# A longer landing delay in the model that orders a hybrid layer's instructions

## The chip, the cores and the metric

The kernel runs on one core of a Trainium2 chip. Its time is the device time of one execution in microseconds; the times before are three executions with a median of 1792.1 us (1790.23 to 1797.07).

## The reference

One layer of a streaming encoder on a sequence of 1024 rows of width 2048, all in float32:

```python
u = einsum('bsd,de->bse', h, w_in)            # one input projection, 6752 columns
q, k, v, z_attn, q_idx, k_idx, w_idx, z_ssd, xbc, dt_raw = split(u)
# group A: a token indexer scores the admissible keys, each query keeps the 256 best
logits = relu(einsum('bqhd,bsd->bqhs', q_idx, k_idx))
score  = where(admissible, einsum('bqhs,bqh->bqs', logits, w_idx), -inf)
sel    = top_k(score, 256)
o_attn = softmax_attention(q, k[sel], v[sel]) * silu(z_attn)
# group B: state-space mixer in chunks of 64 rows, behind a causal convolution of 4 taps
o_ssd  = ssd_mixer(conv(xbc), z_ssd, dt_raw)
sub = einsum('bse,ed->bsd', concat(o_attn, o_ssd), w_out)
h   = layer_norm(alpha * h + sub) * ln_g + ln_b
```

## The kernel before

Matrix products are made in three passes: each float32 operand is split into a high part, rounded to the type fp32r (`xh`, `wh`), and the rest (`xl`, `wl`), and TensorE adds high x high, high x low and low x high. ScalarE writes the high part and VectorE (at times GpSimd) the low part. So each 128x512 tile of raw weights (`wr`) or of x (a tile `u`) takes a transfer, a pass on ScalarE and a pass on VectorE before its matmuls. The two halves of the sequence (512 rows each) go through a Strassen-like scheme of seven products for most of the input projection and for the whole output projection; sums of blocks are formed on VectorE and GpSimd, or by accumulating transfers, and some go through scratch in HBM and come back.

The main stream is a list of weight pieces in fixed order (`units`): the indexer columns, products of the first half, the second, then the output projection (`emit_t`, `emit_s`, `emit_o`). A piece feeds 12 matmuls as a rule. Beside it run tasks: Python generators for rope, indexer scores, top-k search, attention (`t_kv`, `t_attn`: load a piece of q, split it, score, softmax, gate), the state-space mixer (`t_ssd`), splits (`t_w` for weights, `t_x` for x), evacuations, residual sums and the layer norm (`t_lnstat`, `t_ln_one`, `t_ln_b`). A task yields a `Need`: on which engines its next step works, which events it waits for and which buffers it takes.

Nothing in this looks at the chip. While the program is written out, class `Sim` keeps a clock for each engine (`clk`: PE, V, A, G, SP, D for the transfers) and for each tile the times at which its writes and reads end. Whenever the main stream is about to go on, `Flow.pump` looks through the tasks by priority and places the first step that `Flow.ready` allows (lines 442 to 461): the end of its previous step, its events and its buffers must lie behind the clocks of the engines that it needs, with 200 ns of allowance, or 300 ns of margin ahead of TensorE's clock. For that test a transfer ends at the time that `Sim.dma` returns. Engines run their instructions in the order so written, and semaphores keep it right whatever the times are; the model decides only the order. Buffers are handed out by the same clocks (`avail`, `new`, `free`): 10 for raw weights, 4 each for the split ones, 16 each for `xh` and `xl`, 30 of the common kind `u`, of which at most 8 (`NXR`) hold raw x. Weights are split up to 3 pieces ahead (`WAHEAD`) and loaded up to 15 pieces ahead.

Nearly all transfers go out on SP's queue, in the order written; accumulating ones go out on GpSimd's. All instructions are recorded from one helper, so they all carry line 327; tiles tell them apart. In `Sim.dma` a transfer starts 400 ns after its issue or when the transfer clock D is free, keeps D busy for its bytes, and lands a fixed time after that:

## Time and profile before

| | before |
|---|---|
| median of three executions | 1792.1 us |
| profiled execution, its own time | 1794.32 us |
| its span, first to last instruction | 1791.9 us |
| mean granted TensorE clock | 0.972 |
| instructions | 26153 |
| moved by transfers | 430.88 MB, mean 240 GB/s |
| SP's queue, GpSimd's queue | 406.14 MB, 23.07 MB |

The profile shows one execution. Busy time is given by engine (PE is TensorE, PEld its weight loads, DVE VectorE, ACT ScalarE, POOL GpSimd, SP the engine that issues most transfers). A wait is put down to what ended it; a landing is the time at which a transfer's semaphore tells that its data is there. The granted clock is the share of TensorE's full clock.

### The profile page before, as it was taken

The page shows a single profiled execution, that of the slowest core. Times are in us where ns is not written, and L with a number is a line of the kernel's source. Part 1 is how long each engine was busy: PE and PEld are TensorE (multiplying, and loading weights), DVE is VectorE, ACT ScalarE, POOL GpSimd, SP SyncE. Part 2 cuts the span into 40 slices and gives each one's busy share as a digit, 9 for nine tenths or more (in the row PEclk, how much of TensorE's full clock was granted, in tenths as well). Part 3 has the DMA queues.
Part 4 walks back from the last instruction along what each step waited for, and adds up shares of the span by engine and source line. Part 5 has one row for each costly group of instructions (what it writes and reads, how often), then busy time and mean ns, then how long its engine had stood idle before and what let it go on. Part 6 is the DMA issues. An engine that isn't in the chain of part 4 may idle for free. (4 is left out here: it accounts for less than half of the span.)

```text
span 1791.9 us, 26153 instructions
## 1 busy us (share of the span) xinstructions
PE 1656.9 (92%) x7989; PEld 1351.7 (75%) x7989; DVE 1389.1 (78%) x3072; ACT 986.1 (55%) x1920; POOL 231.3 (13%) x300
## 2 busy tenths in 40 slices
PE   7999989999989989889889999999999999899991
PEld 6888867877867878677677888877887788677871
DVE  6888564568899879899776768699886878887775
ACT  6656776555655498876842356465665433333341
POOL 3201012000101000000120223101110000000132
PEclk9999999999999999999899999999999999999996
DMA  9589877596367689987989797686657986767998
GB/s 294 159 299 359 210 223 202 178 311 159 99 222 215 212 274 281 292 240 220 309 240 292 227 295 223 202 286 204 207 179 246 352 285 203 239 194 236 338 244 169
DMA packets 271885, 430.88 MB, mean 240 GB/s; under 512 B 29184, under 2 KB 86912, under 8 KB 271232
## 3 DMA queue, kind: packets, MB, share of 16 engines
q1 hardware_dynamic: 259072, 406.14, 69.0%
q0 software_dynamic: 12672, 23.07, 9.0%
q8 instruction: 63, 1.03, 0.2%
q14 instruction: 78, 0.64, 0.1%
HBM read 337.77 MB, written 131.17 MB: 262 GB/s over the span
## 5 line engine op out<-in xcount | busy, mean ns | idle before, releaser
L327 PE MATMUL pj<-xh,wh 128*128 128x512 f32 (+1 forms) x1520 | 601.1, 395 | 28.2 <-ACT wh L327 25.5
L327 PE MATMUL pj<-xh,wl 128*128 128x512 f32 (+1 forms) x1520 | 591.0, 389 | 20.6 <-DVE wl L327 20.4
L327 PE MATMUL pj<-xl,wh 128*128 128x512 f32 (+1 forms) x1520 | 587.5, 387 | 0.8 <-DVE xl L327 0.4
L327 ACT ACTIVATE wh<-wr 128x512 fp32r<-128x512 f32 (+1 forms) x488 | 298.4, 622 | 236.2 <-PE o L327 79.6
L327 DVE TENSOR_TENSOR wl<-wr,wh 128x512 fp32r<-128x512 f32 (+1 forms) x462 | 314.3, 689 | 143.4 <-ACT wh L327 134.8
L327 PEld LDWEIGHTS pj<-xh,wl 128*128 128x128 f32 x1520 | 290.8, 191 | 89.7 <-DVE wl L327 32.8
L327 PEld LDWEIGHTS pj<-xh,wh 128*128 128x128 f32 x1520 | 291.5, 192 | 85.8 <-ACT wh L327 31.2
L327 PEld LDWEIGHTS pj<-xl,wh 128*128 128x128 f32 x1520 | 291.6, 192 | 52.3 <-DVE xl L327 1.4
L327 PE MATMUL a<-u,u 128*128 128x512 f32 (+3 forms) x776 | 181.6, 355 | 17.4 <-DVE u L327 6.4
L327 DVE TENSOR_TENSOR u<-u,u 128x512 f32<-128x512 f32 (+7 forms) x255 | 156.9, 627 | 48.3 <-ACT u L327 33.6
L327 ACT ACTIVATE u<-u 128x512 f32<-128x512 f32 (+4 forms) x209 | 116.5, 576 | 100.8 <-DVE u L327 46.4
L327 PEld LDWEIGHTS a<-u,u 128*128 128x128 f32 x776 | 129.0, 193 | 53.5 <-DVE u L327 13.5
L327 ACT ACTIVATE u<-s,sm 128x1024 bf16<-128x1024 int16 (+7 forms) x132 | 129.6, 982 | 26.5 <-DVE sm L327 24.9
L327 ACT ACTIVATE xh<-u 128x512 fp32r<-128x512 f32 (+1 forms) x184 | 104.0, 588 | 69.5 <-DVE u L327 25.4
L327 ACT ACTIVATE u<-a 128x256 fp32r<-128x256 f32 (+3 forms) x182 | 61.3, 363 | 142.8 <-DVE u L327 70.4
L327 DVE TENSOR_TENSOR xl<-u,xh 128x512 fp32r<-128x512 f32 (+1 forms) x169 | 109.7, 676 | 36.7 <-ACT xh L327 36.3
L327 PE MATMUL pj<-wh,xh 128*128 128x512 f32 x302 | 125.0, 414 | 8.1 <-DVE s L327 5.2
L327 DVE TENSOR_TENSOR wr<-wr,wr 128x512 f32<-128x512 f32 x173 | 120.5, 697 | 6.0 <-DMA wr<-wt 2.9
L327 PE MATMUL pj<-wl,xh 128*128 128x512 f32 x302 | 119.2, 395 | 1.0 <-DVE wl L327 1.0
L327 PE MATMUL pj<-wh,xl 128*128 128x512 f32 x302 | 119.4, 395 | 0.0
L327 ACT ACTIVATE a<-a 128x512 f32<-128x512 f32 (+3 forms) x160 | 76.1, 505 | 75.4 <-PE a L327 71.1
L327 POOL DMA_DIRECT2D o<-wo x64 | 53.0, 834 | 478.0 <-DMA o<-o 222.7
(154 smaller groups left out, 2066.9 us busy)
## 6 DMA issues: line engine op xcount, KB each, us to landing
wr<-wt SPq DMA_DIRECT2D x424, 256.0 KB, 5.0
u<-xt SPq DMA_DIRECT2D x80, 256.0 KB, 5.7
u<-mx SPq DMA_DIRECT2D x72, 256.0 KB, 5.3
o<-wo POOLq DMA_DIRECT2D x64, 256.0 KB, 6.3
u<-x SPq DMA_DIRECT2D x64, 256.0 KB, 5.4
wr<-o SPq DMA_DIRECT2D x64, 256.0 KB, 4.4
pt<-u SPq DMA_DIRECT2D x48, 256.0 KB, 2.8
u<-pt SPq DMA_DIRECT2D x48, 256.0 KB, 4.9
```

Source lines behind the costliest of these rows:

```text
L327: f(*args, **kw)
```

## The change

In `Sim.dma` the fixed time from the end of a transfer on clock D to its landing is 3400 ns in place of 1500 for transfers issued by SP (and by ScalarE's queue, which the kernel does not use for data). GpSimd's 2000 ns stay, and so does the transfer clock itself. What is computed stays as it is; the order of the instructions on the engines and queues, the buffers that they get, and for some element-wise passes the choice between VectorE and GpSimd (`Flow.pick`) follow from the model.

```diff
         x = max(start + 400, self.clk["D"])
         self.clk["D"] = x + max(out.size(), in_.size()) * 4 * (1 / 352 + 0.35 / row) * (2.0 if eng == "G" else 1.2 if in_dram(out) and in_dram(in_) else 1.0)
-        cell = [self.clk["D"] + (2000.0 if eng == "G" else 1500.0), start]
+        cell = [self.clk["D"] + (2000.0 if eng == "G" else 3400.0), start]
         self.note(notes, cell, "D")
         return cell
```

## The prediction

> **What bounds the kernel now.** I read the totals first, then busy time by window (columns: window, its length, then busy time and count for TensorE, its weight loads, VectorE, ScalarE and GpSimd, granted clock, DMA share, GB/s).

> ```profile
> PE 1656.9 (92%) x7989; PEld 1351.7 (75%) x7989; DVE 1389.1 (78%) x3072; ACT 986.1 (55%) x1920; POOL 231.3 (13%) x300
> ...
> 0.00:1755.80 1755.80, 1656.92 (x7989) 1351.75 (x7989) 1371.47 (x3042) 981.46 (x1914) 221.41 (x288) 0.98 0.78 242
> 1755.80:1792.00 36.20, 0.00 (x0) 0.00 (x0) 17.68 (x31) 4.67 (x6) 9.89 (x12) 0.55 0.78 152
> ```

> TensorE is the bound until 1755.8 us and stands still for 1755.8 - 1656.9 = 98.9 us of that; a tail of 36.2 us without a matmul follows. An order of instructions can move only those two, and the clock. Next the waits: who stood still, for whom, in total, how often, at most.

> ```profile
> PE pj L327 <- ACT wh L327: 25.5, 12, 5.8
> PE pj L327 <- DVE wl L327: 21.4, 20, 3.4
> ACT u L327 <- DMA u<-q: 22.2, 12, 7.1
> ACT xh L327 <- DMA u<-xt: 19.7, 16, 6.6
> DVE u L327 <- DMA u<-mx: 4.8, 3, 2.1
> ```

> TensorE almost never waits for a transfer itself; it waits for ScalarE and VectorE, which split each raw tile into a high and a low part. Those two run strictly in the order written, and they do wait for transfers. So a landing that the order counted on too early stops an engine, and whatever lies behind it comes late to TensorE.

> How early the order counts on it: a 256 KB tile on an idle queue is 0.4 (issue) + 262144 x (1/352 + 0.35/2048) ns = 0.79 + 1.5 = 2.69 us from issue to landing by the model before, 4.59 us after. The measured medians (KB each, us from issue to landing):

> ```profile
> wr<-wt SPq DMA_DIRECT2D x424, 256.0 KB, 5.0
> u<-xt SPq DMA_DIRECT2D x80, 256.0 KB, 5.7
> pt<-u SPq DMA_DIRECT2D x48, 256.0 KB, 2.8
> q<-u SPq DMA_DIRECT2D x16, 256.0 KB, 2.2
> ```

> The loads are 2.3 to 3.0 us later than the model before has it, 0.4 to 1.1 us later than the model after; some stores are as quick as the model before says.

> Then the timeline, for stops of TensorE behind such a landing (start, length, engine, what; in brackets the idle time before and who ended it). The last group is a stop of the other kind, with no transfer in it.

> ```profile
> 242.53 1.28 ACT L327 ACTIVATE u<-u 128x256 fp32r<-128x256 f32 x3 [4.50 <-DMA u<-q]
> 243.00 0.44 PE L327 MATMUL a<-u,u 128*128 128x128 f32 x2 [2.68 <-ACT u L327]
> 243.71 1.13 ACT L327 ACTIVATE wh<-wr 128x512 fp32r<-128x512 f32 x2
> 245.77 0.48 PE L327 MATMUL a<-u,u 128*128 128x128 f32 x1 [2.33 <-DVE u L327]
> ...
> 273.61 0.42 ACT L327 ACTIVATE u<-u 128x256 fp32r<-128x256 f32 x1 [1.53 <-DMA u<-q]
> 274.08 1.21 PE L327 MATMUL a<-u,u 128*128 128x256 f32 x5 [1.64 <-ACT u L327]
> ...
> 856.51 1.42 DVE L327 TENSOR_TENSOR wr<-wr,wr 128x512 f32<-128x512 f32 x2 [2.51 <-DMA wr<-wt]
> 858.66 1.33 PE L327 MATMUL a<-u,u 128*128 128x384 f32 x3 [2.40 <-DVE sm L327]
> ...
> 1548.42 0.69 DVE L327 TENSOR_TENSOR u<-u,u 128x512 f32<-128x512 f32 x1 [1.88 <-DMA u<-mx]
> 1551.02 0.50 PE L327 MATMUL pj<-wh,xh 128*128 128x512 f32 x1 [2.48 <-DVE s L327]
> ...
> 1173.94 0.50 PE L327 MATMUL pj<-xh,wh 128*128 128x512 f32 x1 [1.71 <-ACT wh L327]
> ...
> 1642.70 0.47 PE L327 MATMUL pj<-wh,xh 128*128 128x512 f32 x1 [1.69 <-DVE s L327]
> ...
> 629.54 0.82 ACT L327 ACTIVATE u<-s,sm 128x640 bf16<-128x640 int16 x1
> 630.48 1.15 ACT L327 ACTIVATE u<-s,sm 128x1024 bf16<-128x1024 int16 x1
> 632.30 0.80 PE L327 MATMUL pj<-xh,wh 128*128 128x512 f32 x1 [5.77 <-ACT wh L327]
> ```

> At 242.53 ScalarE has waited 4.50 us for a piece of q; two weight splits stand behind it (243.71), and TensorE stops twice. At 856.51 VectorE has waited 2.51 us for a weight block. At 632.30 the split simply comes after passes of the top-k search.

> A stop has a second price, in the clock column:

> ```profile
> 244.00:251.00 7.00, 5.23 (x17) 4.62 (x18) 6.43 (x21) 4.00 (x9) 1.00 (x2) 0.51 0.84 208
> 274.50:278.00 3.50, 3.50 (x15) 3.17 (x15) 1.98 (x7) 0.05 (x1) 0.85 (x1) 0.55 0.73 126
> 858.60:862.00 3.40, 3.34 (x9) 2.85 (x10) 3.33 (x12) 2.81 (x6) 0.00 (x0) 0.50 0.91 272
> 862.00:878.00 16.00, 16.00 (x74) 12.90 (x72) 11.09 (x28) 14.30 (x30) 3.60 (x5) 1.00 0.99 328
> 1551.50:1554.90 3.40, 3.40 (x10) 2.62 (x9) 3.07 (x6) 0.83 (x2) 1.50 (x2) 0.50 0.74 208
> ```

> After each of these stops TensorE runs at half clock for about 3.4 us (6.8 us after the double one), so half of 3.4 = 1.7 us is lost again. At full clock a matmul takes 16.00/74 = 0.216 us. [...]

> **The change, part by part.** No computation, transfer or wait is added or removed (an element-wise pass may go to GpSimd in place of VectorE or back, which I cost at nothing: VectorE does nearly all of them); the only price is position. (1) Every step that the model holds until a landing is placed 1.9 us of modelled time later on its engine: 1.9/0.216 = about 9 matmuls, or some three VectorE passes of 0.7 us. The instructions behind it move ahead. I count for each stop the smaller of 1.9 us and the wait for the transfer. 243.00 and 245.77: 1.9 + 1.9 = 3.8. 274.08: 1.5. 858.66: 1.9. 1551.02: 1.9. 1173.94 and 1642.70 have only short waits for transfers ahead of them; 0.5 each. Sum 10.1 us. Clock: four stretches of 3.4 us at half speed go, 4 x 1.7 = 6.8 us (of the double one at 244 I count half). Together 16.9 us. What is late next at these places is the other engine: VectorE is at 78% and takes up the slack.

> (2) What moves forward meets other work, and what moves back may itself be late: the price is bounded by zero below and, above, by every one of these stops coming back elsewhere (16.9 us). I take three new stops of 2.0 us, which is near the mean of the waits for a weight split (25.5/12 = 2.1): 6 us.

> (3) Buffers come free later by the model, so loads on SP's queue are placed later too. Weight blocks have ten raw buffers and a block feeds 12 matmuls, 12 x 0.216 = 2.6 us; ten cover about 26 us, far over 5.0 us of landing, so I cost it at nothing. If that cover were gone (a product that takes three raw blocks at once), each such place would cost up to a landing beyond the model, 5.0 - 2.69 = 2.3 us. GpSimd's queue keeps its own 2.0 us; its accumulating transfers change place only with their neighbours, with 13% of the span busy: nothing.

> (4) The tail. Its end hangs on two late loads of finished rows:

> ```profile
> 1773.64 0.77 SPq L327 DMA_DIRECT2D u<-h  x1
> ...
> 1776.20 0.81 ACT L327 ACTIVATE u<-u,mv 128x512 f32<-128x512 f32 x1 [11.74 <-DMA u<-h]
> 1780.95 0.81 ACT L327 ACTIVATE u<-u,mv 128x512 f32<-128x512 f32 x1 [3.94 <-DMA u<-h]
> ```

> One tile more or less left for after the last matmul is worth 1780.95 - 1776.20 = 4.75 us. Either sign is possible, because these loads wait for free buffers and for their turn on SP; I take zero and keep 4.75 us both ways.

> Sum: -16.9 + 6 = -11 us. The profiled execution took 1794.3 us (span 1791.9), 2.2 us over the median of the runs shown; so 1783.3 on that execution, 1781 on the median.

> **The rivals.** (a) Hidden anyway: what the landings cost is taken up by the other kind of stop. For it: the two largest entries of TensorE's waits name splits, and the longest (5.77 us at 632.30) has no transfer near. Then the 10.1 + 6.8 us only change their place, and the time is 1792 less or more a few us: 1785 to 1797. That the change does next to nothing falls in here too.

> (b) Slower: with later landings a split is placed too near its matmul. The place is the weight and x splits. Today 32 stops wait for a weight split (12 + 20) and cost 46.9 us, 1.5 us each. Splits may run three blocks ahead, 3 x 2.6 = 7.8 us; giving up 1.9 us of this brings more of them under zero. If the stops become a third more (11 x 1.5 = 16 us) and five of them trip the clock (5 x 1.7 = 8.5 us), against half of the gain kept (8.5 us), the time is 1792 + 16 = 1808; it decides from about ten new stops on. For it: stores of q and pt land in 2.2 and 2.8 us, near the model before. Against it: all the loads that splits hang on take 5 us or more.

> [...]

> (c) The tail alone moves: 4.75 us, 1787 to 1797.

> **How the numbers follow.** The loads, whose landings hold the splits, are measured near the new constant, and each stop named has its landing in view: 0.46 for the forecast (its own range 1766 to 1783). Rival (a) 0.22, (b) 0.24, (c) 0.08. Half a percent, 9 us, is about what measurement can tell here. Faster is the forecast, 0.46; same is (a) and (c), 0.30; slower is (b), 0.24. The range runs from the whole 16.9 us, one tail tile (4.75) and one double stop such as that at 244 gone in full (0.4 + 0.8 + 3.4 us more than counted), 1792 - 17 - 5 - 4 = 1766, to the price of (b), 1808.

> **What would show it.** Right: ScalarE's waits for u<-q and u<-xt fall by a third or more (22.2 and 19.7 us); TensorE stands still for under 92 us before its last matmul; fewer half-clock stretches. Rival (b): waits of pj for wh and wl grow beyond 46.9 us while waits for transfers shrink. Rival (a): waits for transfers shrink and the 98.9 us stay. Wrong altogether: waits for transfers do not shrink, which would mean that loads are issued later along with their users, the SP queue being held by buffers, not by the model.

## The result, and the profile after

The changed kernel takes 1768.95 us (median of four, 1763.96 to 1771.95) against 1791.16 us for the kernel before beside it: a ratio of 0.9869, 95% interval 0.9834 to 0.9904. A second measurement on another occasion gave 0.9881 (0.9856 to 0.9907); one of its four executions fell into a slower state (1853.3 us) and is left out. The forecast was 1781 us, 11 us less than before, so the time went the forecast way by twice the forecast amount.

The totals and busy time by window after the change, cut at the end of the last matmul (columns as before: TensorE, its weight loads, VectorE, ScalarE, GpSimd, granted clock, DMA share, GB/s):

```profile
PE 1647.6 (93%) x7989; PEld 1352.3 (76%) x7989; DVE 1388.5 (79%) x3058; ACT 980.5 (55%) x1916; POOL 251.3 (14%) x314
...
0.00:1737.80 1737.80, 1647.61 (x7989) 1352.28 (x7989) 1371.88 (x3031) 977.48 (x1912) 243.71 (x305) 0.98 0.79 245
1737.80:1768.80 31.00, 0.00 (x0) 0.00 (x0) 16.63 (x28) 3.04 (x4) 7.63 (x9) 0.55 0.71 156
```

The profiled execution took 1770.57 us, 23.75 less than the one before, and its span is 23.1 us shorter. The two windows divide that. TensorE stands still 1737.8 - 1647.6 = 90.2 us in place of 98.9: -8.7. The same 7989 matmuls keep it busy for 1647.6 us in place of 1656.9: -9.3. The tail without a matmul is 31.0 in place of 36.2 us: -5.2.

The waits after the change, the rows that answer to those shown of before:

```profile
PE pj L327 <- DVE wl L327: 32.8, 17, 4.9
PE pj L327 <- ACT wh L327: 20.1, 9, 4.9
...
ACT xh L327 <- DMA u<-xt: 13.5, 10, 7.6
ACT u L327 <- DMA u<-q: 5.8, 6, 1.7
...
DVE u L327 <- DMA u<-mx: 3.1, 3, 2.3
```

ScalarE waits 5.8 us for pieces of q, where it had waited 22.2. All rows of the waits of ScalarE and VectorE that end on a transfer add up to 184 us before and 100 us after. Beside q, the largest falls are in ScalarE's waits for finished rows (h; 15.7 of their 26.4 us lay in the tail) and for pieces of k, while those for v grew. Before, then after:

```profile
ACT u L327 <- DMA u<-h: 26.4, 6, 11.7
ACT u L327 <- DMA u<-k: 22.3, 4, 7.8
ACT u L327 <- DMA u<-v: 8.9, 3, 3.8
```

```profile
ACT u L327 <- DMA u<-v: 17.2, 3, 8.4
ACT u L327 <- DMA u<-k: 10.1, 3, 8.4
ACT u L327 <- DMA u<-h: 1.8, 4, 0.7
```

TensorE's waits for a weight split went the other way: 25.5 + 21.4 = 46.9 us in 32 stops before, 32.8 + 20.1 = 52.9 us in 26 stops after. All its other standing still fell from 98.9 - 46.9 = 52.0 to 90.2 - 52.9 = 37.3 us.

The loads land nearly as they did; the transfer list of the changed kernel still has 5.0 us for a weight block and 5.5 us (5.7) for a tile of x:

```profile
wr<-wt SPq DMA_DIRECT2D x424, 256.0 KB, 5.0
u<-xt SPq DMA_DIRECT2D x80, 256.0 KB, 5.5
```

So it is the order that changed. The timeline after at the first of the stops that the prediction named, and at one of the longest new stops:

```profile
246.28 0.42 ACT L327 ACTIVATE u<-u 128x256 fp32r<-128x256 f32 x1 [1.69 <-DMA u<-q]
246.75 1.12 PE L327 MATMUL a<-u,u 128*128 128x128 f32 x6 [1.52 <-ACT u L327]
...
737.22 0.81 ACT L327 ACTIVATE u<-s,sm 128x640 bf16<-128x640 f32 x1
...
738.16 1.15 ACT L327 ACTIVATE u<-s,sm 128x1024 bf16<-128x1024 f32 x1
...
739.61 1.41 DVE L327 TENSOR_TENSOR wr<-wr,wr 128x512 f32<-128x512 f32 x2
...
741.11 0.63 ACT L327 ACTIVATE wh<-wr 128x512 fp32r<-128x512 f32 x1 [1.71 <-DVE wr L327]
...
741.76 0.77 PE L327 MATMUL pj<-xh,wh 128*128 128x512 f32 x1 [4.69 <-ACT wh L327]
```

Where ScalarE had stood 4.50 us for a piece of q and TensorE stopped twice (2.68 and 2.33 us), it now stands 1.69 us and TensorE stops once, for 1.52. At 741.76 a split comes behind two passes of the top-k search and behind a sum of weight blocks on VectorE: a stop of the kind that has no transfer in it, and longer than any one of those that the change removed.

The tail after the change:

```profile
1739.29 1.52 ACT L327 ACTIVATE u<-u,mv 128x512 f32<-128x512 f32 x2 [2.56 <-DVE mv L327]
1741.92 1.52 ACT L327 ACTIVATE u<-u,mv 128x512 f32<-128x512 f32 x2 [1.11 <-DVE mv L327]
```

Before, ScalarE's last passes stood at 1776.20 and 1780.95 behind two late loads of finished rows. Here no such load is left: ScalarE is through with the rows of the first half before the last matmul, and its last eight passes, from 1731.62 on, are all for rows of the second half.

### The profile page after: what moved, and what is told of

Read it like the earlier page. It is cut to its first block, busy times and chain, and to the rows that moved or that the text cites. A ratio compares the mean times of both kernels' runs of the same rounds, so it can differ in the third digit from the quotient of the medians.

```text
span 1768.8 us, 26185 instructions
## 1 busy us (share of the span) xinstructions
PE 1647.6 (93%) x7989; PEld 1352.3 (76%) x7989; DVE 1388.5 (79%) x3058; ACT 980.5 (55%) x1916; POOL 251.3 (14%) x314
## 4 chain that ended last, share of the span: by engine, by line
PE 57%; DVE 19%; DMA 10%; issue 6%; ACT 6%; SPq 1%; POOL 1%; DVEq 0%; POOLq 0%; ACTq 0%
PE pj L327 43%; DVE u L327 10%; PE a L327 8%; PE o L327 6%; DMA wr<-wt 3%; ACT u L327 3%; DVE wl L327 3%; DVE s L327 2%; DVE wr L327 2%; ACT wh L327 1%; DMA u<-mx 1%; DVE xl L327 1%; DMA wr<-ws 1%; DMA u<-q 1%; SPq L327 1%
## 5 line engine op out<-in xcount | busy, mean ns | idle before, releaser
L327 PE MATMUL pj<-xh,wh 128*128 128x512 f32 (+1 forms) x1520 | 599.5, 394 | 24.5 <-ACT wh L327 20.1
L327 PE MATMUL pj<-xh,wl 128*128 128x512 f32 (+1 forms) x1520 | 589.5, 388 | 32.5 <-DVE wl L327 32.1
L327 PE MATMUL pj<-xl,wh 128*128 128x512 f32 (+1 forms) x1520 | 587.2, 386 | 1.9 <-DVE xl L327 1.5
L327 ACT ACTIVATE wh<-wr 128x512 fp32r<-128x512 f32 (+1 forms) x488 | 299.6, 623 | 264.8 <-PE pj L327 94.0
L327 DVE TENSOR_TENSOR wl<-wr,wh 128x512 fp32r<-128x512 f32 (+1 forms) x458 | 315.8, 700 | 125.4 <-ACT wh L327 121.8
L327 PEld LDWEIGHTS pj<-xh,wl 128*128 128x128 f32 x1520 | 290.8, 191 | 99.7 <-DVE wl L327 43.3
L327 PEld LDWEIGHTS pj<-xh,wh 128*128 128x128 f32 x1520 | 291.1, 192 | 80.9 <-ACT wh L327 26.1
L327 PEld LDWEIGHTS pj<-xl,wh 128*128 128x128 f32 x1520 | 291.4, 192 | 53.5 <-DVE xl L327 2.5
L327 PE MATMUL a<-u,u 128*128 128x512 f32 (+3 forms) x776 | 178.7, 352 | 8.0 <-DVE u L327 3.7
L327 ACT ACTIVATE u<-u 128x512 f32<-128x512 f32 (+4 forms) x209 | 116.6, 575 | 97.6 <-DVE u L327 54.6
L327 DVE TENSOR_TENSOR u<-u,u 128x512 f32<-128x512 f32 (+8 forms) x253 | 156.6, 633 | 15.5 <-ACT u L327 6.5
L327 PEld LDWEIGHTS a<-u,u 128*128 128x128 f32 x776 | 129.5, 190 | 42.1 <-DVE u L327 10.0
L327 ACT ACTIVATE u<-s,sm 128x1024 bf16<-128x1024 int16 (+7 forms) x132 | 129.7, 983 | 18.8 <-DVE sm L327 15.7
L327 ACT ACTIVATE u<-a 128x256 fp32r<-128x256 f32 (+3 forms) x182 | 61.4, 364 | 135.2 <-PE a L327 68.5
L327 DVE TENSOR_TENSOR xl<-u,xh 128x512 fp32r<-128x512 f32 (+1 forms) x170 | 109.8, 680 | 29.3 <-ACT xh L327 28.6
L327 ACT ACTIVATE xh<-u 128x512 fp32r<-128x512 f32 (+1 forms) x184 | 101.1, 585 | 49.9 <-DVE u L327 19.8
L327 PE MATMUL pj<-wh,xh 128*128 128x512 f32 x302 | 124.7, 413 | 3.0 <-ACT xh L327 1.4
L327 DVE TENSOR_TENSOR wr<-wr,wr 128x512 f32<-128x512 f32 x163 | 114.6, 704 | 9.5 <-DMA wr<-wt 6.8
L327 PE MATMUL pj<-wh,xl 128*128 128x512 f32 x302 | 119.5, 396 | 1.6 <-DVE xl L327 1.6
L327 PE MATMUL pj<-wl,xh 128*128 128x512 f32 x302 | 119.2, 395 | 0.7 <-DVE wl L327 0.7
L327 ACT ACTIVATE a<-a 128x512 f32<-128x512 f32 (+3 forms) x160 | 75.9, 505 | 68.7 <-PE a L327 58.7
L327 POOL DMA_DIRECT2D o<-wo x64 | 53.0, 842 | 390.6 <-DMA o<-wo 205.8
## 6 DMA issues: line engine op xcount, KB each, us to landing
wr<-wt SPq DMA_DIRECT2D x424, 256.0 KB, 5.0
u<-xt SPq DMA_DIRECT2D x80, 256.0 KB, 5.5
u<-mx SPq DMA_DIRECT2D x72, 256.0 KB, 5.0
o<-wo POOLq DMA_DIRECT2D x64, 256.0 KB, 6.4
u<-x SPq DMA_DIRECT2D x64, 256.0 KB, 5.4
wr<-o SPq DMA_DIRECT2D x64, 256.0 KB, 4.0
pt<-u SPq DMA_DIRECT2D x48, 256.0 KB, 3.2
u<-pt SPq DMA_DIRECT2D x48, 256.0 KB, 5.0
```

The lines of the kernel that those rows point to most:

```text
L327: f(*args, **kw)
```

## The experiments

All kernels differ from the kernel before in one expression of `Sim.dma`. Two theories stood at first. Theory 1: the old order counted on landings too early, and the gain is the waits for transfers that go. Theory 2: any change of the constant deals the order anew, and the gain was a good deal. In the tables, the ratio is to the kernel before on the same chip; last matmul, tail and waits (ScalarE and VectorE for transfers, all rows added) are those of each kernel's one profiled execution, in us.

| constant for SP, ns | ratio (95%) | profiled time | last matmul ends | tail | waits for transfers |
|---|---|---|---|---|---|
| 1400 | 1.0041 (1.0026 to 1.0056) | 1795.0 | 1754.7 | 38.3 | 183 |
| 1500 (before) | 1 | 1794.3 | 1755.7 | 36.2 | 184 |
| 1600 | 1.0045 (1.0021 to 1.0068) | 1801.4 | 1758.6 | 40.9 | 176 |
| 2400 | 0.9986 (0.9963 to 1.0010) | 1778.2 | 1745.3 | 30.7 | 121 |
| 3300 | 0.9881 (0.9863 to 0.9899) | 1769.6 | 1732.7 | 35.1 | 75 |
| 3400 (the change) | 0.9869 (0.9834 to 0.9904) | 1770.6 | 1737.7 | 31.1 | 100 |
| 3400, again | 0.9881 (0.9856 to 0.9907) | 1763.9 | 1731.2 | 31.0 | 106 |
| 3500 | 0.9937 (0.9922 to 0.9952) | 1776.9 | 1741.8 | 33.3 | 93 |
| 4300 | 1.0005 (0.9981 to 1.0029) | 1794.0 | 1749.9 | 42.1 | 95 |
| 4400 | 1.0061 (1.0036 to 1.0086) | 1795.1 | 1762.3 | 31.0 | 76 |

| 3400 ns only for | ratio (95%) | profiled time | last matmul ends | tail | waits for transfers |
|---|---|---|---|---|---|
| transfers into SBUF | 0.9949 (0.9927 to 0.9970) | 1767.7 | 1726.1 | 39.8 | 116 |
| the same, 3300 ns | 1.0001 (0.9979 to 1.0022) | 1782.8 | 1739.8 | 41.2 | 121 |
| loads other than raw weights | 0.9969 (0.9948 to 0.9990) | 1776.8 | 1734.9 | 40.0 | 115 |
| transfers into HBM | 1.0002 (0.9983 to 1.0021) | 1789.5 | 1752.3 | 35.4 | 195 |

**Is it luck?** First a small step from the kernel before, then the neighbours of both.

```diff
-(2000.0 if eng == "G" else 1500.0)
+(2000.0 if eng == "G" else 1600.0)     # and 1400.0, 3300.0, 3500.0
```

> The constant goes from 1500 to 1600 ns only. Theory 1 (the order counted on landings too early; the gain is the waits of ScalarE and VectorE for transfers that go): a twentieth of the step, so 1 us of gain, time 1786 to 1794 us, waits for transfers on the two engines near the 184 us of before. Theory 2 (any small change deals the order anew and the gain was luck): the time moves by 8 us or more either way, though the model hardly changed.

> 1400 ns, a neighbour of the kernel before on the low side (1600 took 0.45% longer). Theory 1: waits for transfers near 190 us, time 1788 to 1795 us. Theory 2: anywhere from 1775 to 1800 us, while the waits for transfers stay near 184 us.

> The changed kernel (3400 ns) once more, beside its neighbours on one chip. Both theories: 1764 to 1773 us, about 1.0 to 1.4% under the kernel before.

> 3300 ns, a neighbour of the change. Theory 1 (landings counted on in time): the model differs by 100 ns of 1900, so 1764 to 1776 us, with waits of ScalarE and VectorE for transfers near 100 us. Theory 2 (each constant deals the order anew; of the change's 22 us most is luck): 1778 to 1795 us, with the same waits near 100 us.

> 3500 ns, the neighbour on the other side. Theory 1: 1764 to 1776 us. Theory 2: anywhere from 1765 to 1797 us, with no likeness to 3300 or 3400, though the waits of ScalarE and VectorE for transfers stay near 100 us.

Each step of 100 ns does deal the order anew: comparing the sequences of ScalarE's instructions by operation, tiles (without numbers) and shape, 3300 and 3400 match in 63%, 1500 and 1600 in 63%, 1500 and 3400 in 58%. So neighbours share hardly more of their order than distant constants do. Yet 1400, 1500 and 1600 lie at 1.000 to 1.0045, and 3300, 3400 and 3500 at 0.987 to 0.994. The means of the two groups are 1.003 and 0.990 (0.9875 taken for 3400). The difference, 1.3%, is two to three times the scatter inside a group (up to 0.45 and 0.6%). 1600 and 1400 moved by 0.4% (6 and 7 us; theory 2 had named 8 or more for 1600) where theory 1 expected about nothing, and their intervals leave 1 out: I put that down to the deal. 3300 and 3400 came out as theory 1 expected; 3500, at the top of its range, lies 0.6% off for no reason that the model names. So the level near 3400 is more than one lucky order, and about a third of a percent on either side is luck.

The two groups can also be compared term by term, with one profile of each kernel and two of the changed one:

| in us | 1400, 1500, 1600 | 3300, 3400 (twice), 3500 |
|---|---|---|
| TensorE's waits for weight splits | 40.8 to 56.4 | 43.5 to 52.9 |
| its other standing still before the last matmul | 45.2 to 60.4 | 32.5 to 40.6 |
| its busy time | 1653.5 to 1657.0 | 1646.6 to 1649.8 |
| half clock before the last matmul | 68.3 to 78.5 | 61.4 to 71.7 |
| tail | 36.2 to 40.9 | 31.0 to 35.1 |

Three terms part the groups: standing still apart from weight splits, busy time, and the tail. The waits for weight splits and the half-clock times overlap.

**Loads or stores?** The constant split by where the transfer lands.

```diff
+(2000.0 if eng == "G" else 1500.0 if in_dram(out) else 3400.0)                                  # loads
+(2000.0 if eng == "G" else 3400.0 if in_dram(out) else 1500.0)                                  # stores
+(2000.0 if eng == "G" else 1500.0 if in_dram(out) else 3300.0)                                  # loads, 3300
+(2000.0 if eng == "G" else 1500.0 if in_dram(out) or out.tensor.name.startswith("wr") else 3400.0)  # loads but weights
```

> 3400 ns for transfers that land in SBUF, 1500 ns for those that land in HBM. Theory 1: loads are what the splits wait for, so at least two thirds of the gain stays: 1767 to 1776 us, waits of ScalarE and VectorE for transfers near 100 us as after the change. Theory 2: a new draw, anywhere from 1765 to 1795 us.

> The other part: 3400 ns for transfers that land in HBM, 1500 ns for loads. Theory 1: no more than a third of the gain, 1784 to 1794 us, waits of ScalarE and VectorE for transfers near 184 us. Theory 2: a new draw, anywhere from 1765 to 1795 us, and as likely under 1780 as the loads alone.

> 3300 ns for transfers into SBUF, 1500 ns for those into HBM; a neighbour of the kernel with 3400 for loads alone, which had 0.9949. Theory 1: the loads carry most of the gain, 0.985 to 0.997, 1761 to 1783 us. Theory 2: 1.000 or more.

> 3400 ns only for loads into tiles other than the raw weights (x, pieces of q, k, v, sums put by, state-space inputs, rows); weights and transfers to HBM stay at 1500. If those loads, whose users stand in tasks and come at short notice, carry the gain: 0.987 to 0.997. If the weight blocks do: 0.998 to 1.005, with waits for wr in view and those for u gone.

By time alone the answer is half a yes: loads gave 0.5%, less than the two thirds expected, and nothing at 3300, where theory 2 had 1.000 or more; loads but weights gave 0.3%, at the upper end of what was expected if those loads carry the gain; stores alone gave nothing, as theory 1 expected. The windows tell more. Loads, loads but weights, and stores, each cut at its last matmul:

```profile
0.00:1726.10 1726.10, 1642.42 (x7989) 1349.37 (x7989) 1364.08 (x3009) 966.76 (x1903) 265.08 (x317) 0.99 0.79 246
1726.10:1765.90 39.80, 0.00 (x0) 0.00 (x0) 19.05 (x34) 5.37 (x7) 10.73 (x13) 0.54 0.79 165
```

```profile
0.00:1734.90 1734.90, 1647.69 (x7989) 1354.33 (x7989) 1374.41 (x3024) 977.20 (x1909) 238.88 (x302) 0.98 0.79 245
1734.90:1774.90 40.00, 0.01 (x1) 0.00 (x0) 19.38 (x34) 5.37 (x7) 10.76 (x13) 0.55 0.81 166
```

```profile
0.00:1752.30 1752.30, 1650.60 (x7989) 1354.47 (x7989) 1366.02 (x3017) 977.53 (x1910) 254.29 (x314) 0.98 0.79 243
1752.30:1787.70 35.40, 0.00 (x1) 0.00 (x0) 16.77 (x29) 4.66 (x6) 9.85 (x12) 0.54 0.76 149
```

With the loads late in the model, the last matmul ends at 1726 to 1740 us, about where it does with the whole change (1738 and 1731); with the stores late it ends near where it did before. The profiled execution of the loads kernel is its quickest of ten, 9.6 us under its median, so I shift each figure by what its execution lies off its median, on the estimate that all of this lies ahead of the last matmul, and compare with the kernel before shifted to its own median beside that run. The last matmul then ends 16 us (1736.1 against 1752.5) and 18 us (1731.6 against 1749.6) earlier with the change, 13.5 us earlier with loads (1735.7 against 1749.2), 6.5 with loads at 3300 (1740.0 against 1746.5), 9.3 with loads but weights (1737.2 against 1746.5) and 1.7 us later with stores (1750.9 against 1749.2). By these the loads bring a third to four fifths of what the change brings ahead of the last matmul, and loads other than raw weights, taken alone, fall within that; three orders are too few to say it closer.

What the loads kernels lose is the tail: 39.8 to 41.2 us in place of 31. The tail of the loads kernel, ScalarE and then SP:

```profile
1738.87 0.81 ACT L327 ACTIVATE u<-u,mv 128x512 f32<-128x512 f32 x1 [6.35 <-DMA u<-h]
1754.52 0.81 ACT L327 ACTIVATE u<-u,mv 128x512 f32<-128x512 f32 x1 [14.83 <-DMA u<-h]
```

```profile
1734.29 10.34 SPq L327 DMA_DIRECT2D out<-u  x5
1744.72 0.45 SPq L327 DMA_DIRECT2D u<-h  x1
```

One load of a finished tile of the first half is issued at 1744.72, behind five stores of the result that wait in SP's queue, 10.34 us long, for VectorE. ScalarE starts on it 9.8 us later, and then VectorE and GpSimd finish that one tile. Loads but weights has the same pattern; loads at 3300 has another long tail, of 41.2 us, with no such load in it. A late load of rows stands in the tails of 1400, 1500, 1600 and of stores alone too; with 3300 to 3500 for all transfers none does. Whether a long tail belongs to late loads with early stores, or is a matter of the deal, these runs do not tell.

**Half of the step, and beyond it.**

```diff
+(2000.0 if eng == "G" else 2400.0)     # and 4400.0, 4300.0
```

> 2400 ns, half of the step. By now 1400, 1500 and 1600 lie within 0.45% of each other, and 3300, 3400, 3500 at 0.9881, 0.9881, 0.9937 of before. Theory 1 (a level that follows the landings, with 0.3% of scatter from the order): half of the gain, ratio 0.990 to 0.999, 1770 to 1787 us, waits of ScalarE and VectorE for transfers between 100 and 170 us. Theory 2 (3300 to 3500 share a lucky order; elsewhere nothing is gained): 1.000 to 1.005, 1788 to 1797 us, with waits fallen all the same.

> 4400 ns in place of 3400. A 256 KB tile then lands by the model 5.59 us after its issue, above the 5.0 to 5.7 us measured. Theory 1: waits for transfers fall further, below 100 us, time 1762 to 1772 us. A model that is too late (the rival of the prediction): 1780 us or more, with more stops of TensorE for weight splits. Theory 2: a new draw, 1765 to 1795 us, with no tie to the waits.

> 4300 ns, neighbour of 4400 (ratio 1.006, one stop of 7.9 us behind top-k passes). If above the measured landings the model is too late by rule: ratio 1.000 to 1.010 like its neighbour. If 4400 only drew badly in one stage: 0.985 to 0.996, 1762 to 1781 us. Waits of ScalarE and VectorE for transfers near 76 us in both cases.

At 2400 the waits for transfers fell by 63 us, and the time by 0.14%, at the small end of theory 1; the interval reaches to 1.0010, so no gain at all is not excluded. At 4400 they fell to 76 us, below those of the change, and the kernel is 0.6% slower than before. That is against theory 1 as I first put it, that time follows these waits. ScalarE and then TensorE in the 4400 kernel:

```profile
605.03 0.28 ACT L327 ACTIVATE u<-a 128x128 f32<-128x128 f32 x1 [4.62 <-DVE u L327]
605.20 0.82 ACT L327 ACTIVATE u<-s,sm 128x640 bf16<-128x640 int16 x1
...
606.14 1.15 ACT L327 ACTIVATE u<-s,sm 128x1024 bf16<-128x1024 int16 x1
...
607.29 0.61 ACT L327 ACTIVATE wh<-wr 128x512 fp32r<-128x512 f32 x1
607.81 0.92 ACT L327 ACTIVATE u<-s,sm 128x768 bf16<-128x768 int16 x1
...
608.92 1.04 ACT L327 ACTIVATE u<-s,sm 128x896 bf16<-128x896 int16 x1
...
609.96 0.61 ACT L327 ACTIVATE wh<-wr 128x512 fp32r<-128x512 f32 x1
```

```profile
610.62 0.79 PE L327 MATMUL pj<-xh,wh 128*128 128x512 f32 x1 [7.94 <-ACT wh L327]
```

TensorE stands 7.94 us for the second of two splits, which come among four passes of the top-k search; ScalarE had itself waited 4.62 us for VectorE ahead of these, and no wait for a transfer is in it. TensorE's waits for weight splits are 48.2 us in 33 stops in all, hardly more than before, though more stops had been named as the sign of a model that is too late. The 4300 kernel has no stop of that length there (3.40 us at 605.65), but a tail of 42.1 us. Two kernels beyond 4000 ns gained nothing, which agrees with a model that is too late there; but they lost it at different places, so a common mechanism is not shown.

## Why the prediction was right

**The constant against the landings.** Right in direction, wrong in the account. The 2.69 us that I set against 5.0 to 5.7 hold only when the model's transfer clock is idle, and not all loads that splits hang on take 5 us: `wr<-o` has 4.4 before. When the program of the kernel before is written out, 89% of SP's transfers queue behind clock D, and the time from issue to landing that `Sim.dma` counts for the 1072 loads of 256 KB has a median of 5.23 us; the trace has 5.24. SP's queue runs its 1712 transfers in the order written, so each landing can be set beside the one that was counted on. Of the 1230 loads (transfers into SBUF, of any size), so many came later than that:

| constant for SP, ns | 1500 | 1600 | 2400 | 3300 | 3400 | 3400, again | 4400 |
|---|---|---|---|---|---|---|---|
| loads later than the model | 615 | 554 | 244 | 61 | 73 | 88 | 20 |
| waits for transfers, us | 184 | 176 | 121 | 75 | 100 | 106 | 76 |

So the model before was right in the middle and half of the loads came late; the longer constant turns it into a bound that 6 to 7% of them miss. The three pieces of q issued ahead of the stop at 243.00 were counted on after 5.3 to 5.5 us and took 6.8 to 8.3; after the change they were counted on after 8.5 to 8.6 and took 7.0 to 8.5. Rival (b) had the stores of q and pt for it, at 2.2 and 2.8 us; with its queueing counted, the model before meets the median of the loads too. The rival's time still did not come, for the late half is what ScalarE and VectorE stood waiting for, as in the 4.50 us at 242.53 with two weight splits behind. Fewer late loads go with fewer waits. That the waits alone make the time is not shown: 4400 has the fewest late loads and gained nothing. Making stores later alone changed nothing (1.0002).

**The stops named.** Right in kind, and the sum is too small. Of the seven, one is left with a transfer in view near its old place, at 246.75 and of 1.52 us; another came (1.21 us at 380.56, behind a tile of x for which ScalarE waited 0.42 us). ScalarE's waits for q fell by three quarters, those for x by 31%, just short of the third that was named as the sign. TensorE's standing still apart from weight splits fell by 52.0 - 37.3 = 14.7 us, where 10.1 were counted, and to 32.5 us in the second profile of the changed kernel.

**The price of new stops.** I took 6 us, as three more stops; the waits for weight splits grew by 52.9 - 46.9 = 6.0 us, but in 26 stops, fewer and longer, in place of 32. That the size came out is luck: the same sum is 40.8 us at 1400 and 56.4 at 1600, and 43.5 at 3300, which is as quick as 3400. Neither this price nor rival (b), which had 47 x 1/3 = 16 us, shows above that scatter. Rival (a), that all of it only changes place, fails by the 14.7 us.

**The clock.** 6.8 us were counted, and the runs do not show them. The granted clock's record has 68.3 us at half speed before the last matmul in the profile before, 61.4 in the one after, and 71.7 in the second profile of the changed kernel, whose mean granted clock is 0.972 as before (0.975 in the first) and whose totals are these:

```profile
PE 1646.6 (93%) x7989; PEld 1354.2 (77%) x7989; DVE 1387.5 (79%) x3058; ACT 981.2 (56%) x1916; POOL 250.4 (14%) x314
```

Half of the difference is lost time: 3.4 us less in the one, 1.7 us more in the other. The sign that was named, fewer half-clock stretches, came in one profile of two. TensorE's busy time fell all the same, by 9.3 and 10.3 us, in the second profile nearly all of it at full clock (1584.6 us in place of 1594.6). So a term of about the forecast size came by another way than the one forecast, and what shortened the busy time there stays open.

**The tail.** I took zero and gave 4.75 us either way; it was -5.2. This is the other term that was mis-sized. The two late loads before the end were the thing to price: they were in view. Kernels for which they come before the last matmul have tails of 31.0 (the change, twice, and 4400), 33.3 (3500) and 35.1 us (3300); but 3300 for loads alone has 41.2 without them, so they are not all of it.

Sum by the steps: -10.1 + 6 - 6.8 + 0 = -11 forecast; -14.7 + 6.0 - 9.3 - 5.2 = -23.2 measured in the first pair of profiles. That the forecast was short by half comes from the tail, which was put at zero, from standing still that went beyond the stops named, and from busy time that fell by more than the clock explains.

**What the prediction did not say.** That the change is a deal of the whole order, with a scatter of 0.3 to 0.6% between constants 100 ns apart. Part of the doubled gain may be such a deal: the group near 3400 stands at 1.0% below the kernel before, and the kernel before at 0.3% below the mean of its own group.

## What to carry to other kernels

Where an order is written from a model, set the landing that the model counts on, with its own queueing, beside the measured one, transfer by transfer, and count how many come late: a model that is right in the median is late for half of them. Then look for a compute engine in strict order that waits for a landing with the splits of the next matmuls behind it. Before a gain of one percent from such a constant is believed, run its neighbours: a step that should do nothing shows the scatter, of the time and of each term of it. Price the tail by its own chain, above all a late load that sits in a queue behind stores that wait for something else.

## What the runs showed of the hardware

A stop of TensorE does not always cost clock, and its length alone does not decide. In the profile before, the stop of 1.64 us that ended at 274.08 was followed by a stretch at half clock; after another of 2.15 us, which ended at 412.75, the clock stayed full:

```profile
412.80:416.20 3.40, 3.40 (x19) 2.50 (x19) 2.05 (x6) 1.07 (x3) 0.00 (x0) 1.00 0.22 77
274.90:278.30 3.40, 3.40 (x15) 3.01 (x14) 1.66 (x7) 0.00 (x0) 0.69 (x1) 0.50 0.77 137
```
